# Seven products in place of eight for seven of eight k-tile pairs of up, with up and down woven job by job

## The chip, the cores and the metric

One core of one Trainium2 chip. Times are microseconds on the device from the start to the end of one execution. The kernel's matrix work is on TensorE; VectorE and ScalarE prepare its operands and take its results out of PSUM; SyncE's queue issues the loads of the weights. In rows of the profile TensorE is PE (its weight loads PEld), VectorE DVE, ScalarE ACT, SyncE SP.

## The reference

One layer over 256 tokens of width 2048, in float32: a joint projection feeds differential attention and RWKV-7 mixing, an output projection adds to the residual stream, and then the MLP, which alone the change touches:

```python
h2 = rms_norm(x, norm_mlp[l])
u = jnp.square(jax.nn.relu(jnp.einsum('btd,df->btf', h2, mlp_up[l])))
x = x + jnp.einsum('btf,fd->btd', u, mlp_down[l])
```

`mlp_up` is 2048 x 8192, `mlp_down` 8192 x 2048.

## The kernel before

**Jobs.** All weights go through one stream of jobs. A job is 256 rows of a weight matrix by 512 columns (512 KB): `load` (line 502) takes it into one of four tiles `raw`, `split` (line 517) makes two float32r tiles of it, `hi` (a cast on ScalarE) and `lo = raw - hi` (VectorE), three buffers each. A matrix product in full precision is then three float32r products: hi by hi, hi by lo, lo by hi. Two of these operands are of the activations, which are split in the same way (`hN`, `u`). The list `jobs` (lines 481 to 499) is the order in which jobs are loaded, split and used.

**A group** (`gemm`, line 571) makes 512 columns of the result for all 256 tokens. A group of up has eight jobs, a group of down four. A plain, slow job takes, for each of two k-tiles and two token tiles, three products of 512 columns: twelve.

**Fast jobs.** In groups 3 to 15 of up (`QUICK = 3`) the pairs of k-tiles in `FAST` take the 2 x 2 block form with seven products in place of eight (`seven`, line 545): the weights of a pair are four blocks of 256 columns, VectorE makes four sums and differences of them in the tile `T` (lines 533 to 535: one instruction of 512 elements, two of 256), ScalarE casts them to `Th`, VectorE makes `Tl = T - Th` of 1024, and of `lo` only 256 and 512 elements are needed. The sums of the activations, `S`, are made once, in `normal_h` (line 1449). A fast job is seven times three products of 256 columns, 21. Its partial sums lie in four banks of PSUM (b0 to b3, 512 columns each) instead of two, and `join` (line 1483) puts them together on VectorE, by way of the SBUF tiles `q` and `C`, when the group is over.

**After a group.** For up, ScalarE and VectorE apply the relu while moving 32 x 32 blocks into `z` (line 1500); `fin`, in the next group, transposes, squares and splits it into `u`. For down, VectorE adds the two banks into the residual tile `x2` (line 1393).

**Order.** Before, up and down alternate by groups: one group of up (eight jobs), two of down (four each), and so on (lines 1545 to 1549); each group takes its banks alternately from the tags `acc` and `side` (line 574), four banks each. The program is recorded, and `plan` (line 195) sets a fixed order of each engine's instructions by a list schedule: what can start first goes first, then what has the lowest rank. The rank is the place in the recording, less `SPL = 120` for `split`.

Of the kernel before, what the change touches and what calls it, by code (L numbers as in the profile page):

```python
# [21 lines left out]
P = 128  # L22
# [10 lines left out]
NRAW = 4  # L33
LOOK = 2
EV = 13
FAST = (1, 2, 4, 5, 7)
QUICK = 3

SPL = 120
# [297 lines left out]
def record(ctx, tc, A, nc):  # L337
# [37 lines left out]
    def bank(tag):  # L375
        return ps.tile([P, 512], F32, tag=tag if tag == "acc" else "side", bufs=4, name=nm(tag))
# [99 lines left out]
                advance(t)  # L476

    w_in, w_out, w_up, w_dn = A["w_in"], A["w_out"], A["up"], A["down"]
    turn = [0]

    jobs = []
    cols = [(c + 512 * h, 512) for h in range(2) for c in (4096, 3072, 5120)] + [(c + 512 * h, 512) for h in range(2) for c in (0, 1024, 2048)]
# [5 lines left out]
    def up_jobs(i):  # L488
        return [(w_up, 256 * k, 512 * i, 512) for k in range(8)]
# [1 line left out]
    def fast(job):  # L491
        return job[0] is w_up and job[2] >= 512 * QUICK and job[1] // 256 in FAST

    jobs += up_jobs(0) + up_jobs(1)
    for e in range(8):
        for j in range(4):
            if e < 7 and not j % 2:
                jobs += up_jobs(2 * e + 2 + j // 2)
            jobs += [(w_dn, e * 1024 + 256 * k, 512 * j, 512) for k in range(4)]
    raws, parts = deque(), deque()  # L500

    def load(between=None):
# [42 lines left out]
    def seven(acc, u, k, S, B, first, last):  # L545


        hi, lo, Th, Tl = B
        lt, rt = slice(0, 256), slice(256, 512)

        def a(t, kk):
            return [u[:, i, k + kk, t * P:(t + 1) * P] for i in range(2)]

        def s(i):
            return [S[:, j, i] for j in range(2)]

        def b(kk, n):
            return [x[:, kk, n * 256:n * 256 + 256] for x in (hi, lo)]

        def t(i):  # L560
            return [x[:, i] for x in (Th, Tl)]
        for n, half, x, y in ((2, lt, a(0, 0), b(0, 0)), (0, lt, a(0, 1), b(1, 0)), (0, rt, s(3), b(1, 1)), (3, lt, s(0), t(0)),
                              (3, rt, s(2), t(1)), (2, rt, s(1), t(2)), (1, lt, a(1, 1), t(3))):
            o = acc[n][:, half]
            begin = first and n > 1 and half == lt
            end = last and (n == 1 or half == rt)
            nc.tensor.matmul(o, x[0], y[0], start=begin, stop=False, skip_group_check=True)
            nc.tensor.matmul(o, x[0], y[1], start=False, stop=False, skip_group_check=True)
            nc.tensor.matmul(o, x[1], y[0], start=False, stop=end, skip_group_check=True)

    def gemm(units, w, c0, ncols, evac, side=False, hooks={}, off=0):
        turn[0] += w is w_up or w is w_dn
        quick = [j for j in range(8) if fast((w, 256 * j, c0))]
        acc = [bank("side" if turn[0] % 2 else "acc") for _ in range(4 if quick else 2)]
        nu = 4 if w is not w_out and w is not w_dn else 2
        nh = 2 * nu
        for j in range(nh):
            assert jobs[pos[2]][0] is w and jobs[pos[2]][2:] == (c0, ncols)
            pos[2] += 1
            hi, lo, *T_ = parts.popleft()  # L580
            split()
            if j in hooks:
                hooks[j]()
            if side:
                pump(BD * ncols / 512, BA * ncols / 512)
            if j in quick:
                seven(acc, units[j // 2], 2 * j % 4, sums_[FAST.index(j)], (hi, lo, *T_), j == quick[0], j == quick[-1])
                done(2)
                continue
            for kk in range(2):  # L590
                k = 2 * j + kk
                u = units[off + j // 2]
                for t in range(2):
                    xh = u[:, 0, k % 4, t * P:(t + 1) * P]
                    xl = u[:, 1, k % 4, t * P:(t + 1) * P]
                    o = acc[t][:, :ncols]
                    more = dict(skip_group_check=True) if quick else {}
                    nc.tensor.matmul(o, xh, hi[:, kk, :ncols], start=(k == 0), stop=False, **more)
                    nc.tensor.matmul(o, xh, lo[:, kk, :ncols], start=False, stop=False, **more)
                    nc.tensor.matmul(o, xl, hi[:, kk, :ncols], start=False, stop=(k == 2 * nh - 1), **more)  # L600
        evac(acc)

    def rsqrt_small(out, ss, scale, bias):

# [827 lines left out]
        squares(x2[j], parts2, j)  # L1432

    rows2 = []

    def rstd_rows():

# [11 lines left out]
    def normal_h(j):  # L1449

        u, a = unit("hN"), hA[j]
        hN.append(u)
        for kk in range(4):
            nc.vector.scalar_tensor_tensor(a[:, kk], a[:, kk], pc("g_mlp", 4 * j + kk), rows2[0], op0=ALU.mult, op1=ALU.mult)
        nc.scalar.copy(u[:, 0], a)
        nc.vector.tensor_sub(u[:, 1], a, u[:, 0])
        for p in range(2):
            if 2 * j + p in FAST:

                S, sr = ftile([P, 2, 4, P], "S", F32R), ftile([P, 4, P], "sr")  # L1460
                a1, a2 = a[:, 2 * p], a[:, 2 * p + 1]
                nc.vector.tensor_add(sr[:, 0], a1[:, P:], a2[:, P:])
                nc.vector.tensor_sub(sr[:, 1], sr[:, 0], a1[:, :P])
                nc.vector.tensor_sub(sr[:, 2], a1[:, :P], a1[:, P:])
                nc.vector.tensor_sub(sr[:, 3], a2[:, :P], sr[:, 1])
                nc.scalar.copy(S[:, 0], sr)
                nc.vector.tensor_sub(S[:, 1], sr, S[:, 0])
                sums_.append(S)
                done()
        done()  # L1470
# [6 lines left out]
    us = []  # L1477
    pend = []

    def up_group(i, hooks):  # L1480


        def join(acc):

            C, q = ftile([P, 2, 512], "C"), ftile([P, 3, 256], "q")
            lt, rt = slice(0, 256), slice(256, 512)
            b0, b1, b2, b3 = acc
            nc.scalar.copy(q[:, 0], b2[:, lt])
            nc.vector.tensor_add(q[:, 2], q[:, 0], b2[:, rt])
            nc.vector.tensor_add(q[:, 1], q[:, 2], b3[:, lt])  # L1490
            qf = q.rearrange("p a c -> p (a c)")
            nc.vector.tensor_add(C[:, 0], qf[:, :512], b0)
            nc.vector.tensor_add(C[:, 1, lt], q[:, 2], b1[:, lt])
            nc.vector.tensor_add(C[:, 1, rt], q[:, 1], b1[:, rt])
            nc.vector.tensor_add(C[:, 1, lt], C[:, 1, lt], b3[:, rt])
            nc.vector.tensor_add(C[:, 1, rt], C[:, 1, rt], b3[:, rt])
            done()
            return C

        def f(acc):  # L1500
            z = ftile([P, 4, 2, 4, 32], "z")
            C = join(acc) if i >= QUICK else None
            for t in range(2):
                for tb in range(4):
                    rows = slice(32 * tb, 32 * tb + 32)
                    src = (C[:, t] if C is not None else acc[t]).rearrange("p (f c i) -> p f c i", c=4, i=32)
                    for cb in range(4):
                        o, s = z[32 * cb:32 * cb + 32, :, t, tb, :], src[rows, :, cb, :]
                        r = rstd2[rows, t:t + 1]
                        if 4 * tb + cb < EV:  # L1510
                            nc.scalar.activation(o, s, AF.Relu, **({} if i > 1 else dict(scale=r)))
                        elif i > 1:
                            nc.vector.tensor_scalar(o, s, 0.0, None, op0=ALU.max)
                        else:
                            nc.vector.tensor_scalar(o, s, r, 0.0, op0=ALU.mult, op1=ALU.max)
            if C is not None:
                done()

            def fin():
                u = unit("u")  # L1520
                us.append(u)
                uf = ftile([P, 4, T], "uf")
                nc.vector.transpose(uf.rearrange("p f t -> p (f t)"), z.rearrange("p f t b i -> p (f t b i)"))
                nc.scalar.activation(uf, uf, AF.Square)
                nc.scalar.copy(u[:, 0], uf)
                nc.vector.tensor_sub(u[:, 1], uf, u[:, 0])
                done(2)
            pend.append(fin)
        gemm(hN if i > 1 else hT, w_up, 512 * i, 512, f, hooks=hooks)

    def store_evac(j):
        def f(acc):
# [6 lines left out]
        while pend:  # L1539
            pend.pop(0)()  # L1540

    up_group(0, {2: lambda: make_h(3), 4: rstd_rows})
    up_group(1, {2 * j: lambda j=j: normal_h(j) for j in range(4)})
    done()
    for e in range(8):
        for j in range(4):
            if e < 7 and not j % 2:
                up_group(2 * e + 2 + j // 2, {1: fin_hook})
            gemm(us, w_dn, 512 * j, 512, store_evac(j) if e == 7 else add_evac(x2[j]), hooks={1: fin_hook}, off=2 * e)


def _constants(par):
# [87 lines left out]
```

## Time and profile before

| | us |
|---|---|
| median of 3 runs | 1191.91 (1191.9 to 1193.7) |
| the profiled execution | 1192.01 |
| its span in the trace | 1190.2 |
| TensorE busy | 1179.4 (99%) |
| VectorE busy | 974.1 (82%) |
| ScalarE busy | 844.8 (71%) |

The span is from the first to the last instruction of the program; the execution's time has 1.8 us more around it. Busy time is the union of an engine's records. Records of TensorE and VectorE overlap their successors, so the price of an instruction in a dense run is the distance from its start to the next one's. The weight stream begins with the projections; group 0 of up follows at about 490 us, and from there to the end the MLP runs. All instructions have the line of the helper that emits them (L334), so they are told apart by the tiles they write and read.

### The profile page before, as it was taken

How to read it: one execution, taken by the hardware profiler on the slowest of the kernel's cores; microseconds unless marked ns; L12 is line 12 of the kernel's file. 1: busy time of each engine (PE TensorE's matmuls, PEld its weight loads, DVE VectorE, ACT ScalarE, POOL GpSimd, SP SyncE). 2: the span in 40 equal slices, each digit the busy share in tenths (PEclk: the TensorE clock that was granted, in tenths of full speed). 3: DMA queues.
4: the chain of work that ended last, by engine and by line, in shares of the span. 5: the costliest groups of instructions: out<-in, count | busy, mean ns of one | idle time of the engine just before them, and what ended most of it. 6: DMA issues, size and time to landing. Idle time of an engine off the chain costs nothing.

```text
span 1190.2 us, 18141 instructions
## 1 busy us (share of the span) xinstructions
PE 1179.4 (99%) x6649; PEld 979.9 (82%) x6649; DVE 974.1 (82%) x1579; ACT 844.8 (71%) x1421; POOL 7.3 (1%) x31
## 2 busy tenths in 40 slices
PE   9999999999999999999999999999999999999998
PEld 6887887888778778788888888888888888888886
DVE  7789594896975976798988988988988998898864
ACT  7784566855687768999686777687677677677652
POOL 2000000000000000000000000000000000000000
PEclk9999999999999999999999999999999999999999
DMA  8655656256455445656666666666666666666663
GB/s 279 205 159 164 172 162 184 85 165 175 128 169 172 141 142 184 180 169 194 188 198 199 184 203 198 194 190 197 212 176 196 198 192 182 208 180 197 207 205 132
DMA packets 126297, 216.20 MB, mean 182 GB/s; under 512 B 21824, under 2 KB 24384, under 8 KB 126208
## 3 DMA queue, kind: packets, MB, share of 16 engines
q1 hardware_dynamic: 126208, 215.05, 60.0%
q8 instruction: 52, 0.85, 0.3%
q14 instruction: 37, 0.30, 0.1%
HBM read 211.09 MB, written 3.93 MB: 181 GB/s over the span
## 4 chain that ended last, share of the span: by engine, by line
PE 77%; DVE 10%; ACT 7%; DMA 3%; issue 3%; SPq 0%; DVEq 0%; ACTq 0%
PE acc L334 47%; PE side L334 23%; DVE lo L334 4%; PE sm L334 3%; PE tr L334 3%; ACT z L334 2%; ACT hi L334 2%; DVE Tl L334 2%; DVE T L334 2%; PE sm L179 2%; DMA raw<-up 1%; DMA raw<-w_in 1%; DVE x L334 1%; DVE uf L334 0%; DVE u L334 0%
## 5 line engine op out<-in xcount | busy, mean ns | idle before, releaser
L334 DVE TENSOR_TENSOR lo<-raw,hi 128x1024 fp32r<-128x1024 f32 (+3 forms) x460 | 462.7, 1015 | 151.3 <-ACT hi L334 148.7
L334 ACT CAST hi<-raw 128x1024 fp32r<-128x1024 f32 (+2 forms) x395 | 405.0, 1033 | 164.2 <-PE acc L334 106.8
L334 PE MATMUL acc<-hi,xT 128*128 128x512 f32 (+1 forms) x832 | 267.6, 396 | 0.6 <-ACT hi L334 0.6
L334 PEld LDWEIGHTS acc<-hi,xT 128*128 128x128 f32 x832 | 154.6, 190 | 33.8 <-ACT hi L334 1.7
L334 PE MATMUL acc<-lo,xT 128*128 128x512 f32 (+1 forms) x416 | 164.0, 394 | 0.7 <-DVE lo L334 0.6
L334 PE MATMUL acc<-hi,u 128*128 128x512 f32 x512 | 163.2, 395 | 0.0
L334 PE MATMUL side<-hi,u 128*128 128x512 f32 x512 | 163.1, 395 | 0.0
L334 ACT ACTIVATE z<-C 32x128 f32<-32x128 f32 x338 | 104.2, 308 | 39.4 <-DVE C L334 35.0
L334 ACT CAST Th<-T 128x1024 fp32r<-128x1024 f32 x65 | 68.2, 1050 | 71.0 <-DVE T L334 70.3
L334 PEld LDWEIGHTS acc<-hi,u 128*128 128x128 f32 x512 | 96.4, 188 | 22.4 <-DVE u L334 0.3
L334 PEld LDWEIGHTS side<-hi,u 128*128 128x128 f32 x512 | 96.5, 188 | 22.2
L334 PE MATMUL side<-lo,u 128*128 128x512 f32 x256 | 101.0, 395 | 0.0
L334 PE MATMUL acc<-lo,u 128*128 128x512 f32 x256 | 101.0, 394 | 0.0
L334 PEld LDWEIGHTS acc<-lo,xT 128*128 128x128 f32 x416 | 78.9, 190 | 18.2 <-DVE lo L334 2.2
L334 PE MATMUL side<-hi,hN 128*128 128x512 f32 (+1 forms) x328 | 91.7, 353 | 0.0
L334 PE MATMUL acc<-hi,hN 128*128 128x512 f32 (+1 forms) x308 | 83.4, 343 | 0.0
L334 DVE TENSOR_TENSOR Tl<-T,Th 128x1024 fp32r<-128x1024 f32 x65 | 79.1, 1216 | 0.0
L334 PEld LDWEIGHTS side<-hi,hN 128*128 128x128 f32 x328 | 59.7, 188 | 9.5
L334 PEld LDWEIGHTS acc<-hi,hN 128*128 128x128 f32 x308 | 55.5, 188 | 7.8
L334 PE MATMUL side<-lo,hN 128*128 128x512 f32 (+1 forms) x164 | 57.9, 353 | 0.0
L334 PEld LDWEIGHTS acc<-lo,u 128*128 128x128 f32 x256 | 48.2, 188 | 11.0
L334 PEld LDWEIGHTS side<-lo,u 128*128 128x128 f32 x256 | 48.2, 188 | 11.0
(310 smaller groups left out, 1874.0 us busy)
## 6 DMA issues: line engine op xcount, KB each, us to landing
raw<-up SPq DMA_DIRECT2D x128, 512.0 KB, 3.8
raw<-down SPq DMA_DIRECT2D x128, 512.0 KB, 4.4
raw<-w_in SPq DMA_DIRECT2D x93, 512.0 KB, 3.8
raw<-w_out SPq DMA_DIRECT2D x32, 512.0 KB, 3.9
raw<-w_in SPq DMA_DIRECT2D x8, 288.0 KB, 3.1
x<-x SPq DMA_DIRECT2D x4, 512.0 KB, 7.3
out<-x SPq DMA_DIRECT2D x8, 256.0 KB, 3.4
raw<-w_in SPq DMA_DIRECT2D x6, 256.0 KB, 5.8
```

Of the source, the lines that this page charges most:

```text
L179: p.fn(*p.args, **p.kw)
L334: op.fn(*op.args, **op.kw)
```

## The change

`FAST` grows from five pairs to seven (only pair 0 stays slow). `gemm` becomes a generator, `steps`, which yields after each job, so that two groups can be recorded in turns. From group 3 of up on, the eight jobs of a group of up and the eight of two groups of down follow the string `WEAVE`; down groups lag by one pair less than before, and six of them are left for the end in place of four. All groups of up but the second take their banks from `acc`, all of down from `side`. In `join` two adds of 256 become one of 512, and its instructions get the rank of `split`. `normal_h` makes seven `S`; the first two lie in small tiles that the earlier stages have done with (`HOME`).

```diff
-FAST = (1, 2, 4, 5, 7)
+FAST = (1, 2, 3, 4, 5, 6, 7)
...
-    jobs += up_jobs(0) + up_jobs(1)
-    for e in range(8):
-        for j in range(4):
-            if e < 7 and not j % 2:
-                jobs += up_jobs(2 * e + 2 + j // 2)
-            jobs += [(w_dn, e * 1024 + 256 * k, 512 * j, 512) for k in range(4)]
+    def down_jobs(d):
+        return [(w_dn, d // 4 * 1024 + 256 * k, d % 4 * 512, 512) for k in range(4)]
+
+
+    WEAVE = "ddududuududududu"
+    for i in range(3):
+        jobs += up_jobs(i)
+    for i in range(3, 16):
+        ups, downs = up_jobs(i), down_jobs(2 * i - 6) + down_jobs(2 * i - 5)
+        jobs += [(ups if c == "u" else downs).pop(0) for c in WEAVE]
+    for d in range(26, 32):
+        jobs += down_jobs(d)
...
-    def gemm(units, w, c0, ncols, evac, side=False, hooks={}, off=0):
-        turn[0] += w is w_up or w is w_dn
+    def gemm(*args, **kw):
+        for _ in steps(*args, **kw):
+            pass
+
+    def steps(units, w, c0, ncols, evac, side=False, hooks={}, off=0, tag="acc"):
         quick = [j for j in range(8) if fast((w, 256 * j, c0))]
-        acc = [bank("side" if turn[0] % 2 else "acc") for _ in range(4 if quick else 2)]
+        acc = [bank(tag) for _ in range(4 if quick else 2)]
...
+            if j < nh - 1:
+                yield
         evac(acc)
+        yield
...
+            nc.rank = -SPL
             nc.scalar.copy(q[:, 0], b2[:, lt])
...
-            nc.vector.tensor_add(C[:, 1, lt], C[:, 1, lt], b3[:, rt])
-            nc.vector.tensor_add(C[:, 1, rt], C[:, 1, rt], b3[:, rt])
+            c1 = C[:, 1].rearrange("p (n c) -> p n c", n=2)
+            nc.vector.tensor_add(c1, c1, b3[:, rt].unsqueeze(1).broadcast_to([P, 2, 256]))
+            nc.rank = 0
...
+    def down_group(d):
+        e, j = d // 4, d % 4
+        return steps(us, w_dn, 512 * j, 512, store_evac(j) if e == 7 else add_evac(x2[j]), hooks={1: fin_hook}, off=2 * e, tag="side")
...
+    for i in range(3, 16):
+        gens = {"u": up_group(i, {}), "d": run(down_group(2 * i - 6), down_group(2 * i - 5))}
+        for c in WEAVE:
+            next(gens[c])
+    for _ in run(*(down_group(d) for d in range(26, 32))):
+        pass
```

Where instructions stand now, on VectorE. First, two fast jobs in the middle of a group of up, before (each row: line, operation, tile written and tiles read, shape):

```order
L334 TENSOR_TENSOR T_1395<-raw_1370 128x512
L334 TENSOR_TENSOR Tl_1388<-T_1386,Th_1387 128x1024
L334 TENSOR_TENSOR lo_1391<-raw_1367,hi_1390 128x1024
L334 TENSOR_TENSOR T_1395<-raw_1370,T_1395 128x256
L334 TENSOR_TENSOR lo_1394<-raw_1370,hi_1393 128x256
L334 TENSOR_TENSOR T_1395<-raw_1370,T_1395 128x256
L334 TENSOR_TENSOR lo_1394<-raw_1370,hi_1393 128x512
L334 TENSOR_TENSOR T_1401<-raw_1373 128x512
L334 TENSOR_TENSOR lo_1400<-raw_1373,hi_1399 128x256
L334 TENSOR_TENSOR T_1401<-raw_1373,T_1401 128x256
L334 TENSOR_TENSOR lo_1400<-raw_1373,hi_1399 128x512
L334 TENSOR_TENSOR Tl_1397<-T_1395,Th_1396 128x1024
```

And at the like place in the change:

```order
L334 TENSOR_TENSOR T_1431<-raw_1408 128x512
L334 TENSOR_TENSOR lo_1430<-raw_1408,hi_1429 128x256
L334 TENSOR_TENSOR T_1431<-raw_1408,T_1431 128x256
L334 TENSOR_TENSOR lo_1430<-raw_1408,hi_1429 128x512
L334 TENSOR_TENSOR T_1431<-raw_1408,T_1431 128x256
L334 TENSOR_TENSOR lo_1436<-raw_1414,hi_1435 128x1024
L334 TENSOR_TENSOR T_1440<-raw_1419 128x512
L334 TENSOR_TENSOR Tl_1433<-T_1431,Th_1432 128x1024
L334 TENSOR_TENSOR T_1440<-raw_1419,T_1440 128x256 x2
L334 TENSOR_TENSOR lo_1439<-raw_1419,hi_1438 128x256
L334 TENSOR_TENSOR lo_1439<-raw_1419,hi_1438 128x512
L334 TENSOR_TENSOR lo_1445<-raw_1425,hi_1444 128x1024
```

Before, two fast jobs' T, lo and Tl follow one another; now the lo of a job of down (128x1024, `raw` and `hi` read) stands between them. Next, the end of a group of up, before:

```order
L334 TENSOR_TENSOR lo_1418<-raw_1398,hi_1417 128x1024
L334 TENSOR_TENSOR lo_1426<-raw_1404,hi_1425 128x1024
L334 TENSOR_TENSOR q_1422<-q_1422,side_1382 128x256
L334 TENSOR_TENSOR q_1422<-q_1422,side_1383 128x256
L334 TENSOR_TENSOR C_1421<-q_1422,side_1381 128x256
L334 TENSOR_TENSOR C_1421<-q_1422,side_1380 128x512
L334 TENSOR_TENSOR C_1421<-q_1422,side_1381 128x256
L334 TENSOR_TENSOR C_1421<-C_1421,side_1383 128x256 x2
L334 TENSOR_TENSOR lo_1429<-raw_1407,hi_1428 128x1024
```

And in the change:

```order
L334 TENSOR_TENSOR q_1452<-q_1452,acc_1383 128x256
L334 TENSOR_TENSOR T_1469<-raw_1443 128x512
L334 TENSOR_TENSOR q_1452<-q_1452,acc_1384 128x256
L334 TENSOR_TENSOR C_1451<-q_1452,acc_1382 128x256
L334 TENSOR_TENSOR C_1451<-q_1452,acc_1381 128x512
L334 TENSOR_TENSOR C_1451<-q_1452,acc_1382 128x256
L334 TENSOR_TENSOR T_1469<-raw_1443,T_1469 128x256
L334 TENSOR_TENSOR C_1451<-C_1451,acc_1384 128x512
```

The last adds into C are one instruction of 512, the four banks are all of `acc`, and the T of the next group's first fast job is worked in. Third, the rows that follow these in the change:

```order
L334 TENSOR_TENSOR lo_1459<-raw_1437,hi_1458 128x1024
L334 TENSOR_TENSOR T_1469<-raw_1443,T_1469 128x256
L334 TENSOR_TENSOR T_1478<-raw_1449 128x512
L334 TENSOR_TENSOR T_1478<-raw_1449,T_1478 128x256
L334 TENSOR_TENSOR lo_1468<-raw_1443,hi_1467 128x256
L334 TENSOR_TENSOR lo_1468<-raw_1443,hi_1467 128x512
L334 TENSOR_TENSOR Tl_1471<-T_1469,Th_1470 128x1024
L334 TENSOR_TENSOR T_1478<-raw_1449,T_1478 128x256
L334 TENSOR_TENSOR T_1484<-raw_1457 128x512
```

The four tiles `raw` are used in turn: raw_1457 is loaded four loads after raw_1437 (1437, 1443, 1446, 1449, 1457), into the same place, which the first row here reads last; the last row is the first to read the new one.

## Rows read from the trace of the kernel before

**Rows 1.** Page, first and second part: TensorE's busy time; granted clock by slices.

```profile
PE 1179.4 (99%) x6649; PEld 979.9 (82%) x6649; DVE 974.1 (82%) x1579; ACT 844.8 (71%) x1421; POOL 7.3 (1%) x31
...
PEclk9999999999999999999999999999999999999999
```

**Rows 2.** Stretches: us; busy PE, PEld, DVE, ACT, POOL (instructions); clock, DMA share, GB/s.

```profile
635.10:1068.40 433.30, 432.88 (x2372) 373.33 (x2370) 385.35 (x601) 314.72 (x501) 0.00 (x0) 1.00 0.64 194
...
744.20:770.00 25.80, 25.72 (x156) 22.72 (x155) 25.73 (x40) 16.94 (x19) 0.00 (x0) 1.00 0.62 181
...
770.00:787.00 17.00, 17.00 (x82) 14.12 (x81) 12.23 (x20) 13.86 (x32) 0.00 (x0) 1.00 0.68 215
...
508.00:545.00 37.00, 37.00 (x160) 29.98 (x160) 35.87 (x68) 35.06 (x67) 0.00 (x0) 1.00 0.61 180
```

**Rows 3.** TensorE's timeline: start, us, engine, line, product, shape, count.

```profile
755.87 0.28 PE L334 MATMUL acc<-hi,hN 128*128 128x256 f32 x1
...
758.37 0.39 PE L334 MATMUL acc<-hi,hN 128*128 128x512 f32 x1
...
764.68 0.28 PE L334 MATMUL acc<-Th,S 128*128 128x256 f32 x1
...
765.04 0.39 PE L334 MATMUL acc<-Tl,S 128*128 128x256 f32 x1
...
769.34 0.28 PE L334 MATMUL acc<-lo,hN 128*128 128x256 f32 x1
...
771.69 0.40 PE L334 MATMUL side<-hi,u 128*128 128x512 f32 x1
...
782.84 0.40 PE L334 MATMUL acc<-hi,u 128*128 128x512 f32 x1
```

**Rows 4.** VectorE's timeline, same columns; idle time before and its releaser.

```profile
757.68 0.42 DVE L334 TENSOR_TENSOR T<-raw,T 128x256 f32<-128x256 f32 x1
...
758.01 0.69 DVE L334 TENSOR_TENSOR lo<-raw,hi 128x512 fp32r<-128x512 f32 x1
...
758.62 0.69 DVE L334 TENSOR_TENSOR T<-raw 128x512 f32<-128x512 f32 x1
...
764.90 1.22 DVE L334 TENSOR_TENSOR lo<-raw,hi 128x1024 fp32r<-128x1024 f32 x1
...
766.03 0.42 DVE L334 TENSOR_TENSOR T<-raw,T 128x256 f32<-128x256 f32 x1
...
787.05 0.69 DVE L334 TENSOR_TENSOR T<-raw 128x512 f32<-128x512 f32 x1 [0.82 <-DMA raw<-up]
```

**Rows 5.** VectorE's groups, 635.1 to 1068.4 us: busy, mean ns, idle before.

```profile
L334 DVE TENSOR_TENSOR lo<-raw,hi 128x1024 fp32r<-128x1024 f32 x111 | 134.4, 1218 | 38.7 <-ACT hi L334 38.1
...
L334 DVE TENSOR_TENSOR T<-raw,T 128x256 f32<-128x256 f32 x100 | 41.8, 418 | 0.3
...
L334 DVE TENSOR_SCALAR z<-C 32x128 f32<-32x128 f32 x60 | 13.3, 222 | 1.3
...
L334 DVE STREAM_TRANSPOSE uf<-z 128x1024 f32<-128x1024 f32 x10 | 12.4, 1238 | 0.0
```

**Rows 6.** Waits, 635.1 to 1068.4 us: us in total, times, longest.

```profile
DVE lo L334 <- ACT hi L334: 38.1, 46, 1.8
...
ACT hi L334 <- PE side L334: 13.7, 15, 1.3
...
ACT hi L334 <- PE acc L334: 13.4, 15, 1.3
...
DVE T L334 <- DMA raw<-up: 7.2, 10, 0.9
```

**Rows 7.** ScalarE's groups, 635.1 to 1068.4 us.

```profile
L334 ACT CAST Th<-T 128x1024 fp32r<-128x1024 f32 x50 | 52.5, 1050 | 51.9 <-DVE T L334 51.3
```

**Rows 8.** Page, sixth part: transfers, KB each, median us from issue to landing.

```profile
raw<-up SPq DMA_DIRECT2D x128, 512.0 KB, 3.8
...
raw<-down SPq DMA_DIRECT2D x128, 512.0 KB, 4.4
```

More of the change, by code (lines that the diff above doesn't have):

```diff
@@ L478, in record @@
     w_in, w_out, w_up, w_dn = A["w_in"], A["w_out"], A["up"], A["down"]
-    turn = [0]
     jobs = []
@@ L554, in s @@
         def s(i):
-            return [S[:, j, i] for j in range(2)]
+            return [S[j][:, i] for j in range(2)]
         def b(kk, n):
@@ L588, in gemm @@
                 done(2)
-                continue
-            for kk in range(2):
+            for kk in range(0 if j in quick else 2):
                 k = 2 * j + kk
@@ L1434, in record @@
     rows2 = []
+    HOME = {0: ("DW", "DA"), 1: ("X", "Sp")}
     def rstd_rows():
@@ L1458, in normal_h @@
             if 2 * j + p in FAST:
-                S, sr = ftile([P, 2, 4, P], "S", F32R), ftile([P, 4, P], "sr")
+                sr = ftile([P, 4, P], "sr")
+                if len(sums_) in HOME:
+                    S = [sm.tile([P, 512], F32R, tag=g, bufs=1, name=nm("S")).rearrange("p (s t) -> p s t", s=4) for g in HOME[len(sums_)]]
+                else:
+                    S = ftile([P, 2, 4, P], "S", F32R)
+                    S = [S[:, 0], S[:, 1]]
                 a1, a2 = a[:, 2 * p], a[:, 2 * p + 1]
@@ L1465, in normal_h @@
                 nc.vector.tensor_sub(sr[:, 3], a2[:, :P], sr[:, 1])
-                nc.scalar.copy(S[:, 0], sr)
-                nc.vector.tensor_sub(S[:, 1], sr, S[:, 0])
+                nc.scalar.copy(S[0], sr)
+                nc.vector.tensor_sub(S[1], sr, S[0])
                 sums_.append(S)
@@ L1478, in record, with up_group @@
     pend = []
-    def up_group(i, hooks):
+    def up_group(i, hooks, tag="acc"):
         def join(acc):
@@ L1528, in f @@
             pend.append(fin)
-        gemm(hN if i > 1 else hT, w_up, 512 * i, 512, f, hooks=hooks)
+        return steps(hN if i > 1 else hT, w_up, 512 * i, 512, f, hooks=hooks, tag=tag)
     def store_evac(j):
@@ L1540, in fin_hook, with run @@
             pend.pop(0)()
-    up_group(0, {2: lambda: make_h(3), 4: rstd_rows})
-    up_group(1, {2 * j: lambda j=j: normal_h(j) for j in range(4)})
-    done()
[L1545 to L1549, printed above, removed]
+    def down_group(d):
+        e, j = d // 4, d % 4
+        return steps(us, w_dn, 512 * j, 512, store_evac(j) if e == 7 else add_evac(x2[j]), hooks={1: fin_hook}, off=2 * e, tag="side")
+    def run(*gens):
+        for g in gens:
+            yield from g
+    for _ in run(up_group(0, {2: lambda: make_h(3), 4: rstd_rows}),
+                 up_group(1, {2 * j: lambda j=j: normal_h(j) for j in range(4)}, "side")):
+        pass
+    done()
+    for _ in up_group(2, {1: fin_hook}):
+        pass
+    for i in range(3, 16):
[3 more added lines that the diff above has]
+    for _ in run(*(down_group(d) for d in range(26, 32))):
+        pass
 def _constants(par):
```

## The prediction

> **What bounds the kernel now.** Read the page's first part, then the table by stretches, then TensorE's and VectorE's timelines, then the waits. [...] But the next engine is not far behind: over ten whole periods of the MLP (a period is one group of up and two of down, 16 jobs) VectorE is busy 385.35 of 433.3 us, ScalarE 314.72 [rows 2]. One period takes 43.33 us, of which VectorE works 38.5. It is not even: in the stretch from 744.2 to 770.0, where the five fast jobs of a group stand together, VectorE is busy for 25.73 of 25.8 us; in the next 17 us, under the two groups of down, for 12.23 [rows 2].
>
> TensorE's price of a job is read from starts, since records overlap. A down group of 48 products of 512 columns starts at 771.69 and the next begins at 782.84 [rows 3]: 11.15 us, 0.232 a product, 2.79 a job of twelve. A fast job of 21 products of 256 runs from 755.87 to 758.37, 2.50; from the second product of another, 769.34, to the end of its group at 771.69 are 2.35 for twenty, 2.47 for 21 [rows 3]. I use 2.48, 0.118 a product. 11 slow and 5 fast jobs make 43.09 us; the period is 43.33, so about 0.24 is stall. It is seen where the fast jobs have used up VectorE's lead: the step from 764.68 to 765.04 is 0.36 instead of 0.12 [rows 3].
>
> VectorE too is read from starts: 256 elements step by 0.33, 512 by 0.61, 1024 by 1.13 [rows 4]. A fast job issues T (512), T, T (256 each), lo (256 and 512), Tl (1024): 0.61 + 3 x 0.335 + 0.61 + 1.13 = 3.35 us, against 2.48 on TensorE. A slow job has one lo, 1.13 against 2.79. So VectorE falls behind in up and recovers in down, and its idle time is there: 38.1 us in ten periods waiting for hi, while ScalarE's hi waits 27.1 us for TensorE to give back a hi buffer [rows 6]. That is an engine up to three jobs ahead, with nothing to do.
>
> **The change part by part.** (1) *Two more jobs of each of 13 groups go by seven products.* TensorE saves 2 x (2.79 - 2.48) = 0.62 us a period, 8.1 in all, on the path. The period's floor on TensorE becomes 9 x 2.79 + 7 x 2.48 = 42.47.
>
> [...] The rows show a product of 256 columns at half the price of one of 512, with no fixed part that can be seen [rows 3]. [...]
>
> (2) *VectorE pays for it.* Per converted job lo of 1024 goes and Tl of 1024 comes, so the thousands cancel; added are T and lo of 512 and three of 256: 2 x 0.61 + 3 x 0.335 = 2.22, 4.45 a period. (3) *The join's last two adds become one* of 512: 0.61 for 2 x 0.33, a gain of 0.06. VectorE's work in a period was 38.5 by busy time. By steps it is 17 of 1024 (11 lo, five Tl, one u) x 1.13 = 19.2, 15 of 512 (five T, five lo, four x, one C) x 0.61 = 9.2, 21 of 256 (ten T, five lo, two q, four C) x 0.335 = 7.0, and the transpose and six z at 1.24 + 1.33 [rows 5]: 38.0. Busy time is higher because each dense run ends in a full record. After: 17, 20 and 25 of them, 42.4 by steps, 42.9 by busy time. **VectorE then needs as much as TensorE**, 42.4 against 42.47, and what idles it is on the path.
>
> (4) *The weave.* It adds no work. It sets a lo of 1.13 beside each fast job, 4.48 us of VectorE for 5.27 of TensorE, so that the lead isn't used up in a run of fast jobs; that is what makes 42.4 us of work fit at all. With the lead even, the 0.24 of stall goes, and its place is taken by whatever makes VectorE wait. (5) *ScalarE* gains two Th of 1.05 [rows 7], 2.1 on 31.5 of 43.3: covered by the ten idle us that are left, and Th waited for VectorE 51.9 us in ten periods, so it is not what is late. (6) *The banks.* Every group of up now takes all four banks of acc, so the next group waits for the join. The two down jobs that open a period give 2 x 2.79 = 5.6 us. Between the last fast product and the last read of the first two banks stand one ScalarE copy of 256 columns, under the 1.05 of a cast of 1024 [rows 7], and by the order two q, a T and three C, 2 x 0.335 + 0.61 + 2 x 0.335 + 0.61 = 2.6: 3.6 us at most, covered by 2.0; if the join begins later than that, TensorE stands. (7) *Two more sums of h.* At most 4 x 0.335 + 0.61 = 1.95 each on VectorE, 3.9 together, before the third group of up. From 508 to 545 VectorE had 1.1 us free [rows 2]; the eight slow jobs after that leave it 8 x (2.79 - 1.13). Price 0 to 2; with thirteen free us behind it I take nothing.
>
> (8) *The transfers.* Here is the cost that the trace of before doesn't show. T reads a job's raw tile early, lo reads it last and frees it, and there are four. VectorE waits for raw once a period now, 7.2 us in ten [rows 6], 0.82 at 787.05 [rows 4], where it is idle anyway. In the new order the tightest place is the third piece of VectorE's order above: from the end of lo on the tile four loads earlier to the T that needs the new one stand three T and one lo of 256, T and lo of 512, and one Tl, 4 x 0.335 + 2 x 0.61 + 1.13 = 3.69 us, and the transfer needs 3.8 for up, 4.4 for down from issue to landing [rows 8]. So VectorE waits between 0.1 and 0.7 there; nothing if it stood elsewhere in between. I take 0.35 a period.
>
> **Sum.** VectorE 42.4 + 0.35 = 42.75 us a period against 43.33: 0.58 x 13 = 7.5 us. From the profiled execution's 1192.0 (the median of the runs shown is 0.1 below): **1184.5 us**. At best TensorE's floor holds: 0.86 x 13 = 11.2, about 1180 with rounding. With VectorE at 42.9 and 0.2 of waits it is 0.23 x 13 = 3.0 less, 1189.
>
> **Rivals.** *The raw tiles starve VectorE; slower.* With no idle time left, every late landing counts. Four T of a period have under 5 us of VectorE work to cover their transfer, by the same counting 3.7, 4.4, 4.9 and 5.0. If the landing, in a stream that now changes between two matrices, takes 5.2 us in place of 3.8 to 4.4, those four wait 1.5 + 0.8 + 0.3 + 0.2 = 2.8, less what one wait gives the next, an estimate of 2 us: 44.4 a period, 1.07 x 13 = 14 us more, 1206. It decides at 0.93 us of VectorE idle a period (43.33 - 42.4). For it: landing is already longer than the cover at one place. Against: the queue has moved 512 KB per 2.7 us all along with the DMA engines busy 64% [rows 2]. Chance 0.11.
>
> *Given back; no change.* VectorE's small waits (ScalarE's hi, Th, the join's copy) add up to 0.75 to 1.1 us a period. For it: a static order has to meet two engines at 100%. Against: the dense stretch of 25.8 us with no gap [rows 2]. 1190 to 1194; 0.2%, 2.4 us, is what a measurement of this kernel can tell from no change. Chance 0.08.
>
> *Records, not steps, are VectorE's price; slower.* If each instruction held the engine for its whole record (1.22 for 1024, where the next starts after 1.13 [rows 4]), the work would be 17 x 1.22 + 20 x 0.69 + 25 x 0.42 + 2.6 = 47.6 us a period, 4.3 x 13 = 56 us more, 1248. [...] Chance 0.01.
>
> *Small products cost more between long ones; no change.* Now products of 256 and 512 columns change over every job, not every few. At 2.79 / 21 = 0.133 a product instead of 0.118 a fast job saves nothing. Against: both runs of fast products that gave 2.50 and 2.47 end in such a change [rows 3]. [...] Chance 0.01.
>
> That the change doesn't do what it says is excluded: the order shows the lo of down jobs between the T of up jobs.
>
> **How the numbers follow.** Forecast 0.79, all of it faster by over 0.2%, 1180 to 1189; no change 0.09; slower 0.12. Leaving out the slower cases and a little below the floor: 1179 to 1192.
>
> **What would show it.** Right: periods of 42.5 to 43.0 us, VectorE busy 98% or more in them, few waits of lo for hi, and T waiting for raw as VectorE's main wait. TensorE's steps should be 0.232 and 0.118 as before, with stalls of a few tenths before Tl and lo. Wrong: VectorE idle by over 0.9 us a period, TensorE waiting before the first product of a group of up (the join), or ScalarE's hi late with its buffers free.

## The result, and the profile after

The changed kernel takes **1198.95 us** (median of 6 runs, 1198.2 to 1201.9) against 1191.97 for the kernel before on the same chip: a ratio of 1.0061, 95% interval 1.0047 to 1.0075. It is slower by 7 us, where 7.5 us less was forecast. One of the six executions of the kernel before took 3705.71 us; the ratio goes by the others. The profiled execution's span is 1196.8 us, before 1190.2.

The page's first part of the change, busy times:

```profile
PE 1172.5 (98%) x6883; PEld 983.1 (82%) x6883; DVE 1034.6 (86%) x1706; ACT 875.2 (73%) x1449; POOL 7.3 (1%) x31
```

The table by stretches over ten whole periods of the change, columns as in [rows 2]:

```profile
666.30:1103.80 437.50, 428.16 (x2552) 377.32 (x2550) 429.78 (x691) 336.33 (x521) 0.00 (x0) 1.00 0.62 193
```

A period takes 43.75 us, before 43.33 [rows 2]. VectorE works 42.98 of them, 98.2%, before 38.5; TensorE's clock is whole throughout (1.00). So VectorE is as full as forecast, but TensorE's periods did not get shorter. TensorE's timeline at one place of each period:

```profile
709.35 0.28 PE L334 MATMUL acc<-Tl,hN 128*128 128x256 f32 x1
709.47 0.28 PE L334 MATMUL acc<-Th,hN 128*128 128x256 f32 x1
709.58 0.63 PE L334 MATMUL side<-hi,u 128*128 128x512 f32 x2
711.13 0.50 PE L334 MATMUL side<-lo,u 128*128 128x512 f32 x1 [0.91 <-DVE lo L334]
711.46 0.39 PE L334 MATMUL side<-hi,u 128*128 128x512 f32 x1
711.70 0.39 PE L334 MATMUL side<-lo,u 128*128 128x512 f32 x1
```

Products of 256 columns step by 0.12 and of 512 by 0.23, as in [rows 3]; from 709.58 two products should last 0.46 us, and the third starts after 1.55. It waits for the `lo` of the down job that follows the two neighbouring fast jobs of `WEAVE` ("uu"). The same stall stands in every one of these periods, 1.0 to 1.4 us with the step after it. What VectorE does before it, from its timeline:

```profile
699.54 1.22 DVE L334 TENSOR_TENSOR Tl<-T,Th 128x1024 fp32r<-128x1024 f32 x1
700.77 0.22 DVE L334 TENSOR_SCALAR z<-C 32x128 f32<-32x128 f32 x1
701.02 0.43 DVE L334 TENSOR_TENSOR T<-raw,T 128x256 f32<-128x256 f32 x1
...
704.79 1.22 DVE L334 TENSOR_TENSOR Tl<-T,Th 128x1024 fp32r<-128x1024 f32 x1
705.92 0.42 DVE L334 TENSOR_TENSOR T<-raw,T 128x256 f32<-128x256 f32 x1
706.26 0.68 DVE L334 TENSOR_TENSOR x<-x,side 128x512 f32<-128x512 f32 x1
706.96 0.22 DVE L334 TENSOR_SCALAR z<-C 32x128 f32<-32x128 f32 x1
707.19 0.43 DVE L334 TENSOR_TENSOR T<-raw,T 128x256 f32<-128x256 f32 x1
707.63 0.46 DVE L334 TENSOR_SCALAR z<-C 32x128 f32<-32x128 f32 x2
708.12 0.69 DVE L334 TENSOR_TENSOR x<-x,side 128x512 f32<-128x512 f32 x1
708.73 1.24 DVE L334 STREAM_TRANSPOSE uf<-z 128x1024 f32<-128x1024 f32 x1
709.89 1.19 DVE L334 TENSOR_TENSOR lo<-raw,hi 128x1024 fp32r<-128x1024 f32 x1
```

And ScalarE's timeline there:

```profile
704.50 3.19 ACT L334 ACTIVATE z<-C 32x128 f32<-32x128 f32 x10
707.71 2.00 ACT L334 CAST hi<-raw 128x1024 fp32r<-128x1024 f32 x2
```

VectorE has no gap here; the `lo` at 709.89 comes after six `z` and the transpose. One `z` steps by 0.23 to 0.25, and an instruction ahead of a run of `z` steps 0.1 longer: `Tl` to `z` is 1.23 where `Tl` to `T` is 1.13, `x` to `z` 0.70 where `x` to `uf` is 0.61. Six `z` in four runs cost 0.25 + 0.49 + 0.23 + 0.49 + 4 x 0.1 = 1.86 us (the second run stands at 702.42, not shown). The planner (`plan`, which fixes the order) has a table of costs that gives a `z` 0.068 + 128 x 0.00052 = 0.135, 0.81 for six. VectorE's steps here are not in proportion to the elements: four steps of 256 elements would be 4 x 0.335 = 1.34 us, where one of 1024 is 1.13, and a `z` of 128 takes 0.235.

The change's waits from 650 to 1070 us (in total, times, longest):

```profile
ACT hi L334 <- PE side L334: 56.3, 33, 2.8
...
PEld side L334 <- DVE lo L334: 13.7, 10, 1.6
PE side L334 <- DVE lo L334: 9.3, 10, 1.1
...
DVE lo L334 <- ACT hi L334: 3.9, 9, 0.4
...
DVE T L334 <- DMA raw<-up: 0.2, 1, 0.2
```

And the page's sixth part, median us from issue to landing last:

```profile
raw<-up SPq DMA_DIRECT2D x128, 512.0 KB, 4.5
raw<-down SPq DMA_DIRECT2D x128, 512.0 KB, 4.0
```

`T` waiting for raw, forecast as VectorE's main wait, is all but gone, though tiles of up land later than in [rows 8]. VectorE's own idle time, 0.77 us a period, is for more than half a wait of `lo` for `hi` (4.4 of 7.7 us in the ten periods). That `hi` had waited for TensorE to give back one of three buffers, as VectorE's timeline and then ScalarE's show at one place:

```profile
730.75 2.36 DVE L334 TENSOR_TENSOR lo<-raw,hi 128x1024 fp32r<-128x1024 f32 x2 [0.44 <-ACT hi L334]
```

```profile
729.67 2.12 ACT L334 CAST hi<-raw 128x1024 fp32r<-128x1024 f32 x2 [2.21 <-PE side L334]
```

So the engines wait for each other by turns: TensorE is late, `hi` and `lo` are then late, and what VectorE has lost there it lacks at the next "uu".

Summed over all of TensorE's starts from 440 us on (each distance beyond 0.118 or 0.232, if by more than 0.03), the stalls are 21.0 us, before 6.3: 7.3 against 3.0 up to 650, and 13.6 against 3.3 from there. The products save 8.1. 14.7 - 8.1 = 6.6 us, the difference of the two spans. Of the 4.3 more up to 650, 2.2 stand between 550 and 560, where the first down group waits for `u` (TensorE's timeline below), 1.3 at 570, where a fast job waits, and 2.0 at 621, the same `lo` after "uu" in the second woven period; some 1.2 of stalls that the kernel before had between 575 and 600 are gone:

```profile
553.61 0.40 PE L334 MATMUL acc<-hi,hN 128*128 128x512 f32 x1
555.02 0.50 PE L334 MATMUL side<-hi,u 128*128 128x512 f32 x1 [1.02 <-ACT u L334]
...
556.52 0.73 PE L334 MATMUL side<-hi,u 128*128 128x512 f32 x2 [0.76 <-DVE u L334]
```

### The profile page after: what moved, and what is told of

Same layout as the page of the kernel before. It is cut to its first block, busy times and chain, and to the rows that moved or that the text cites. A ratio compares the mean times of both kernels' runs of the same rounds, so it can differ in the third digit from the quotient of the medians.

```text
span 1196.8 us, 18805 instructions
## 1 busy us (share of the span) xinstructions
PE 1172.5 (98%) x6883; PEld 983.1 (82%) x6883; DVE 1034.6 (86%) x1706; ACT 875.2 (73%) x1449; POOL 7.3 (1%) x31
## 4 chain that ended last, share of the span: by engine, by line
PE 65%; DVE 21%; ACT 7%; issue 5%; DMA 3%; SPq 0%; DVEq 0%; ACTq 0%
PE acc L334 37%; PE side L334 21%; DVE lo L334 8%; DVE T L334 3%; ACT hi L334 3%; PE tr L334 2%; DVE Tl L334 2%; PE sm L334 2%; DMA raw<-up 2%; PE sm L179 2%; DVE C L334 1%; ACT z L334 1%; DVE z L334 1%; DVE uf L334 1%; DVE x L334 1%
## 5 line engine op out<-in xcount | busy, mean ns | idle before, releaser
L334 PE MATMUL side<-hi,u 128*128 128x512 f32 x1024 | 336.5, 395 | 1.8 <-ACT u L334 1.0
L334 PEld LDWEIGHTS side<-hi,u 128*128 128x128 f32 x1024 | 191.9, 188 | 42.6 <-ACT u L334 1.5
L334 PE MATMUL side<-lo,u 128*128 128x512 f32 x512 | 203.3, 397 | 11.8 <-DVE lo L334 11.8
L334 PE MATMUL acc<-hi,hN 128*128 128x256 f32 (+1 forms) x532 | 134.8, 317 | 0.8 <-DVE z L334 0.8
L334 ACT CAST Th<-T 128x1024 fp32r<-128x1024 f32 x91 | 95.2, 1047 | 25.0 <-DVE T L334 24.5
L334 PE MATMUL acc<-Th,S 128*128 128x256 f32 x546 | 112.3, 281 | 0.0
L334 PEld LDWEIGHTS acc<-Th,S 128*128 128x128 f32 x546 | 90.2, 188 | 0.0
L334 PE MATMUL acc<-lo,hN 128*128 128x256 f32 (+1 forms) x266 | 84.3, 317 | 0.0
L334 DVE TENSOR_TENSOR T<-raw,T 128x256 f32<-128x256 f32 x182 | 76.7, 422 | 1.7
L334 PE MATMUL acc<-Tl,S 128*128 128x256 f32 x273 | 77.2, 283 | 0.0
L334 DVE TENSOR_TENSOR T<-raw 128x512 f32<-128x512 f32 x91 | 62.5, 687 | 1.6 <-DMA raw<-up 1.3
```

The lines of the kernel that those rows point to most:

```text
L334: op.fn(*op.args, **op.kw)
```

## The experiments

Stalls below are such sums over TensorE's starts, up to 650 us / from there. In kernels with added lines the helper stands at L338.

| kernel | us | ratio to before, 95% | stalls |
|---|---|---|---|
| change | 1198.95 | 1.0061 (1.0047 to 1.0075) | 7.3 / 13.6 |
| weave5 | 1200.88 | 1.0072 (1.0057 to 1.0087) | 4.5 / 9.5 |
| weave6 | 1213.64 | 1.0182 (1.0167 to 1.0197) | 6.7 / 24.5 |
| plain7 | 1236.63 | 1.0374 (1.0357 to 1.0391) | 12.9 / 45.0 |
| finlate | 1209.87 | 1.0146 (1.0120 to 1.0171) | 8.0 / 20.3 |
| rank_hi | 1197.12 | 1.0038 (1.0024 to 1.0053) | 5.6 / 13.4 |
| uuend | 1199.62 | 1.0060 (1.0045 to 1.0075) | 8.4 / 14.5 |
| uuend_rank | 1200.80 | 1.0066 (1.0049 to 1.0083) | 7.2 / 16.6 |
| weave5_rank | 1200.49 | 1.0069 (1.0045 to 1.0093) | 4.2 / 10.6 |
| meas_z | 1198.97 | 1.0063 (1.0050 to 1.0075) | 5.6 / 15.5 |
| meas_l | 1202.62 | 1.0089 (1.0075 to 1.0103) | 6.6 / 17.8 |
| meas_zl | 1190.97 | 0.9995 (0.9986 to 1.0004) | 7.6 / 5.7 |
| meas_z2l | 1188.70 | 0.9975 (0.9964 to 0.9985) | 5.7 / 4.6 |
| head_s | **1187.60** | 0.9965 (0.9953 to 0.9978) | 4.8 / 5.5 |
| weave5_zl | 1193.47 | 1.0018 (1.0009 to 1.0026) | 3.4 / 3.8 |
| weave6_zl | 1194.87 | 1.0029 (1.0018 to 1.0041) | 4.7 / 7.9 |
| before_zl | 1194.89 | 1.0029 (1.0018 to 1.0040) | 3.0 / 6.0 |
| end_13 | 1188.58 | 0.9973 (0.9963 to 0.9983) | 4.8 / 5.7 |
| end_15 | 1196.39 | 1.0036 (1.0024 to 1.0049) | 4.9 / 12.5 |

**Is VectorE's load the cause?** Three kernels set the number of fast pairs and the order apart: the weave with five pairs and with six, and (plain7) the kernel before with seven pairs and seven `S`, in its order of whole groups.

```diff
-    FAST = (1, 2, 3, 4, 5, 6, 7)
+    FAST = (1, 2, 4, 5, 7)            # weave5
+    FAST = (1, 2, 3, 4, 5, 7)         # weave6
```

> The weave alone: the changed kernel with the five fast pairs of before (1, 2, 4, 5, 7). Theory A, VectorE is full (its 43.0 us of work and 0.75 of idle make the period of 43.75): with 2 x 2.2 us less on VectorE TensorE bounds, 11 x 2.79 + 5 x 2.48 = 43.1 a period, stalls below 0.3, so as before (43.33) or 2 to 3 us better, plus what the start of the weave costs (about 3 us): 1190 to 1194. Theory B, one lo comes late because blocks of z on ScalarE and the transposition uf on VectorE stand ahead of it: the place stays, with a stall near 1.25 a period: 44.3 a period, about 1207.

> One fast pair less than the change, pair 6, whose job lies behind the place of the stall in the period. Theory A (VectorE full): VectorE needs 40.8 us, TensorE 10 x 2.79 + 6 x 2.48 = 42.8, so TensorE bounds: a period of 42.8 to 43.0, stall under 0.3, about 1186 to 1190. Theory B (the late lo alone): VectorE's work ahead of the place is unchanged, the stall of 1.25 stays, period 44.0, about 1202.

> Seven fast pairs in before's order of whole groups (the two more sums of h where the change puts them, before's join). Theory A: VectorE's work is the same 42.5 to 43 us a period, but seven fast jobs in a row need 23.5 us of it for 17.4 of TensorE, and three jobs of lead don't cover 6.1 us: 45 to 47 us a period, 1213 to 1240. If the total alone counted, as in the change: about 1199.

weave5 gives VectorE back the work of two pairs and is no faster than the change; its time lies between what the two theories gave. Its stall stands at the same `lo`, 0.3 to 1.2 us a period. What is new is a wait of `T` for raw at the head of the period, ahead of the rest of the join. SyncE's timeline shows the issue, VectorE's the wait, and the waits from 650 to 1070 us the sum:

```profile
860.88 0.37 SPq L334 DMA_DIRECT2D raw<-up  x1
```

```profile
865.79 0.69 DVE L334 TENSOR_TENSOR T<-raw 128x512 f32<-128x512 f32 x1 [1.14 <-DMA raw<-up]
866.40 0.41 DVE L334 TENSOR_TENSOR q<-q,acc 128x256 f32<-128x256 f32 x1
```

```profile
DVE T L334 <- DMA raw<-up: 29.3, 18, 2.9
```

The tile came 4.9 us after its issue; the planner counts 1.1 + 524288 / 360000 + 0.9 = 3.5. Whatever stands behind that `T` in VectorE's fixed order, the join and by it all `z`, is then 1.1 us late. So a lighter VectorE alone does not help: theory A falls as the sole cause, and the weave costs some 8 us even with five pairs. weave6 is slower by 12 us than either theory allowed; its stall too stands mostly at that `lo`, 1.1 to 1.8 us a period. plain7, as theory A expected, shows what seven pairs cost without the weave, 45 us.

**Is it the work ahead of that one `lo`?** finlate holds the transpose and what follows it for the second down group; rank_hi lets the `split` of woven jobs go before other work; uuend moves the two neighbouring fast jobs to the period's end; uuend_rank has both of the last two edits, weave5_rank has rank_hi's with five pairs.

```diff
+    def held_fin():
+        nc.hold = True
+        fin_hook()
+        nc.hold = False
...
-            nc.rank = -SPL
+            nc.rank = -(SPL if pos[1] <= 160 else 1000)
...
-    WEAVE = "ddududuududududu"
+    WEAVE = "ddududududududuu"
```

> The change with uf, its square and the split into u held back to the second group of down in a period, so that they no longer stand ahead of the lo that TensorE waits for; the work is the same. Theory A: VectorE stays full, a period of 43.0 at best, no more than 0.75 a period better: 1189 to 1198. Theory B: the stall goes, period 42.5 to 42.8, 1183 to 1187.

> The change with the rank of split lowered from -120 to -1000 from the first woven job on, so that whenever a hi, lo, T, Th or Tl can start it goes ahead of z, x, uf and u; the work is the same. Theory C (the first half of a period is overfull: join, z, x, uf and u stand ahead of the parts of the next jobs on ScalarE and VectorE, and a lead of at most three jobs doesn't carry TensorE over it): the order gets better, the stall of 1.25 a period falls to 0.5 or less, 1186 to 1191. Theory D (the fixed order meets the chip's times badly wherever VectorE and ScalarE are near full, whatever goes first): as the change or worse, 1197 to 1212.

> The change with the two neighbouring jobs of up moved from the middle of WEAVE to its end (dd ud ud ud ud ud ud uu). Theory C: the overfull first half loses one fast job's 3.35 us of VectorE in exchange for a lo of 1.13, so the stall there goes; at the end VectorE has no join to do: stall under 0.5 a period, 1186 to 1191. Theory D: the stall comes back at another place, 1197 to 1212.

> Both of the two edits before. Theory C: at or near TensorE's floor where VectorE's 43.0 us allow it, 43.0 a period, 1186 to 1190. Theory D: 1197 to 1212.

> The weave with five fast pairs and the lower rank. VectorE has 4.8 us of slack a period here. Theory C: stall under 0.2, 43.2 a period, 1190 to 1193 with about 2.5 us lost at the start of the weave. Theory D: as the weave with five, 1199 to 1202.

All five stay at 1197 us or above. finlate is slower than either of its theories had it; at 752 us twelve `z` on ScalarE still stand ahead of the `hi` there. rank_hi and uuend move the stall elsewhere, to `Tl` of fast jobs, and its sum stays at 13 to 14.5 us; the waits from 650 to 1070 us of rank_hi:

```profile
PEld acc L334 <- DVE Tl L334: 7.6, 9, 0.9
```

So it is not one unlucky place, and theory D is right for the four kernels that it was set against.

**Do the planner's prices cause it?** The order is fixed before the run by durations in the planner's table. meas_z raises the price of `z` to 0.285, near the rows above, and that of the transpose from 1.13 to 1.24, the length of its record, though it steps by 1.16 there (708.73 to 709.89). meas_l raises the landing of a tile from 3.5 to 4.5, meas_zl does all of it; "both prices" below are VectorE's and the landing. The instructions stay the same; only their order moves.

```diff
+            if fname == "tensor_scalar" and aps[0].shape[0] == 32:
+                self.cost += 0.15
+            if fname == "transpose":
+                self.cost += 0.11
...
-            done = dma + 0.9
+            done = dma + (1.9 if op.ins[0].tensor.name in ("up", "down") else 0.9)
```

> Same work as the change; only two prices by which the kernel's planner lays the fixed order are set to what the trace of the change shows: a z block on VectorE (32x128) 0.28 us in place of 0.135 (it steps by 0.235, and each run of them delays its neighbours by about 0.1), the transpose 1.24 in place of 1.13. Theory E: six z in a period cost VectorE some 1.1 us more than the order allows, all of it ahead of the one lo that has no slack in that order (the down job after the two neighbouring fast jobs), and TensorE's stall of 1.25 us a period is that. An order that knows the price puts other work there: stall below 0.5 a period, period 42.8 to 43.2, total 1187 to 1193. Rival A' (VectorE is simply full: 43.0 us of busy time in a period, whatever the order): stall moves but stays, 43.5 to 43.8, total 1196 to 1200.

> The change with one price of the planner corrected, that of the landing (1.0 us later for tiles of up and down); the z keep their price. Theory L (the order counts on raw tiles that come about 1 us too early; VectorE and ScalarE stand in front of them with other work behind): 1189 to 1193, as meas_zl. Theory ZL (both prices are needed, since VectorE is at 98% and each of the two uses up the slack that the other leaves): 1194 to 1198.

> As meas_z, and the planner also counts the landing of a raw tile 1.0 us later (traces: 4.0 to 4.9 us from issue to landing; the planner counts about 3.5). Theory E: in the change T waited for raw for only 0.2 us in ten periods, so the landing is no cause there: within 2 us of meas_z. If landing matters once the z are priced right, meas_zl is faster than meas_z by 2 us or more.

One price alone gives nothing, or less than nothing; both together give 8 us. The waits from 650 to 1070 us show where the stall went. With `z` alone corrected (meas_z, first rows), VectorE waits for raw, which it did not in the change, where it came late anyway, and TensorE's stall goes over in the main to `hi` and `Th` of fast jobs; with the landing alone (meas_l, second rows), `lo` is as late as before:

```profile
DVE T L338 <- DMA raw<-up: 8.3, 9, 1.4
PEld acc L338 <- ACT hi L338: 5.5, 10, 0.7
...
PEld acc L338 <- ACT Th L338: 3.9, 6, 0.7
...
PEld side L338 <- DVE lo L338: 2.4, 4, 0.7
```

```profile
PEld side L334 <- DVE lo L334: 14.2, 10, 1.4
PE side L334 <- DVE lo L334: 12.1, 10, 1.2
...
DVE T L334 <- DMA raw<-up: 0.8, 2, 0.5
```

Theory E, which held `z` to be enough in the change, falls. Rival A' (VectorE is full whatever the order) has the time of meas_z, but falls with meas_zl, which has the same work. Theory ZL, that both are needed, stands, though meas_l lies 4.6 us above its range. The same two prices on the weave with fewer pairs:

> The weave with five fast pairs, order laid with both corrected prices. Five pairs leave VectorE over 4 us a period, and yet TensorE stalled 0.9 a period: at the head of each period a T stands first on VectorE and waits 1.2 us for raw, and all behind it, the join and the z too, comes 1.2 us late at the one lo without slack. Theory E: with the landing priced right the stall goes: period 43.1 to 43.4, total 1192 to 1195. Rival W (the weave itself costs, by banks, join or rhythm, whatever the order's prices): 1199 or more, as weave5.

> Six fast pairs (without pair 6) in the weave, order laid with both corrected prices. It was 1213.6 with the planner's own prices. Theory E: VectorE needs 40.8 of some 42.8 us, so there is slack: 1187 to 1193. Rival W: 1199 or more.

They gain 7.4 and 18.8 us, and in weave5_zl no wait of `T` for raw is left among the waits from 650 to 1070 us. weave5_zl lies where it was expected, weave6_zl 2 us above. The weave with five or six pairs stays 2 to 3.5 us slower than the kernel before. The control:

> The kernel before with the same two prices corrected, as a control. If the corrected order helps whatever the kernel, this gains too: 1186 to 1190. Theory L says that the order before, where VectorE waits for raw only under down with slack behind it and TensorE stalled 0.24 us a period, has little to win: 1190.5 to 1192.5.

The order before loses 3 us by the corrected prices (for `z` those of meas_z2l, below), more than either expectation had. They are no general cure: the new order brought 2.7 us more of stalls, of TensorE for `Tl`. That it had nothing to win because slack stood behind the waits for raw [rows 4, 6] is likely, but not shown.

**The head.** meas_zl still waits 2.4 us for `u` at 553; there `z` reads PSUM and was priced right before (its steps in meas_zl are 0.32 to 0.39, as at 566.97 and 547.55; the price was 0.36). meas_z2l raises the price for SBUF sources only; head_s lets the sums `S` go later besides.

```diff
-            if fname == "tensor_scalar" and aps[0].shape[0] == 32:
+            if single and aps[0].shape[0] == 32:
...
+                nc.rank = 100
                 sr = ftile([P, 4, P], "sr")
```

> As meas_zl, but the price of z is raised only for blocks read from SBUF; those of the first three groups of up, read from PSUM, step by 0.30 to 0.39 and were right before. In meas_zl TensorE waited 2.6 us at 553 and 1.3 at 577 for u and z of the first groups. Expected: the periods as in meas_zl (42.9 to 43.0), the head 0 to 2 us better, 1188 to 1191.

> As meas_z2l, and the sums S of the activations get a rank 100 places later, so that the split, z and u of the first groups go before them on VectorE. Theory H: the change costs about 4 us at its head (from the first job of group 1 of up to the third woven period), because seven S in place of five are made where VectorE is full; later S let the first down groups have their u in time: 1185 to 1189. Rival: the S are then late for the first fast jobs and the stall only moves: 1189 to 1192.

Both beat the kernel before, by 3 and 4 us. In meas_z2l, ten periods in the table by stretches, and its waits from 650 to 1070 us:

```profile
665.00:1094.60 429.60, 428.43 (x2552) 376.42 (x2550) 425.01 (x690) 333.57 (x521) 0.00 (x0) 1.00 0.62 196
```

```profile
PEld side L338 <- DVE lo L338: 4.0, 10, 0.5
...
DVE T L338 <- DMA raw<-up: 0.6, 2, 0.4
```

The period is 42.96 us and VectorE works 42.50 of it, 0.5 less than in the change with the same instructions: its load too depends on the order. Its `z` stand in three runs a period, in the change in four, which by the rows above is 0.1 of the 0.5; the rest is not explained.

The two intervals overlap, so that the later `S` help is not shown; the stalls up to 650 fell from 5.7 to 4.8, and 3.0 would be as before. But they moved: between 550 and 560, where the first down group waits for `u`, they fell from 2.1 to 0.1 us, and between 560 and 575 they rose from 0.8 to 2.2. The rival to theory H is right for the most part.

**What keeps the last 0.5 us a period?** end_13 is head_s with the neighbouring fast jobs at the end; end_15 differs from it only in four of six `z` that ScalarE takes over.

```diff
-                        if 4 * tb + cb < EV:
+                        if 4 * tb + cb < (EV if i < 3 else 15):
```

> As head_s, with the two neighbouring fast jobs at the end of the period. VectorE has the same work. With both prices right the place of the pair should not matter, since VectorE is the bound: within 2 us of head_s, 1186 to 1190. As uuend against the change (1199.6 and 1198.95).

> As end_13, with four of the six z blocks on VectorE in each period moved to ScalarE from group 3 of up on: VectorE loses 4 x 0.235 and the 0.1 beside each run of them, about 1.1 us a period, ScalarE gains 1.3 on 32.7. If VectorE's load is what keeps the period at 42.96 above TensorE's 42.47 once the order is right, the period falls to 42.5 to 42.7 and the total to 3 to 6 us under end_13. If the rest of the stall is lateness of single transfers or of ScalarE, it stays within 1 us of end_13 or gets worse.

end_13 came as expected: with both prices right the place of the pair doesn't matter, as it did not in uuend. end_15 is slower by 8 us though VectorE has 11 us more of idle time from 650 to 1070 us (busy for 404.29, in end_13 for 415.73). Its stretch and its waits:

```profile
650.00:1070.00 420.00, 414.52 (x2455) 362.86 (x2454) 404.29 (x628) 338.88 (x549) 0.00 (x0) 1.00 0.62 193
```

```profile
PEld acc L338 <- DVE Tl L338: 9.0, 20, 1.2
...
DVE T L338 <- DMA raw<-up: 5.5, 8, 1.3
```

So that VectorE's load is what holds the period at 42.96 is not shown; a lighter VectorE under another order waits again for raw, and TensorE for `Tl`. Every change of a price or of the work lays a new order, and the luck of each order is worth some us. What speaks against luck in the prices is that each of the four woven kernels that was laid both ways gains: 8.0 us (change to meas_zl), 7.4 and 18.8 (five and six pairs), and 11.0 (uuend to end_13, which has the later `S` too); and that all four kernels with seven pairs and both prices and six `z` on VectorE (meas_zl, meas_z2l, head_s, end_13) lie at 1187.6 to 1191.0, and the five that have seven pairs in a weave without both (change, rank_hi, uuend, uuend_rank, finlate) at 1197.1 to 1209.9, as do meas_z and meas_l. No kernel was laid with prices put off the other way, which would tell what a new order alone is worth.

## Why the prediction was wrong, point by point

**(1) held.** Products of 256 columns stepped by 0.118 among products of 512 as well; 8.1 us are saved. The rival of dearer small products is out.

**(2) held in the higher of its two numbers.** VectorE's busy time is 42.98 us a period; by busy time 42.9 was forecast, by steps 42.4. The steps left out that an instruction ahead of a run of `z` takes 0.1 longer: six `z` cost 1.86 in place of 1.33. The sum took the lower number, 0.5 us a period too little for this order. The rival that whole records are VectorE's price, 47.6, is out.

**(3), (5) and (6) held.** No stall of TensorE stands at the first product of a group of up. ScalarE works 33.6 us a period, the 31.5 + 2.1 of the forecast.

**(4) is the step that failed**: "With the lead even, the 0.24 of stall goes, and its place is taken by whatever makes VectorE wait." The lead is not even. In the order as laid, one `lo` a period comes behind all the `z`, the transpose and two of the residual's adds, and TensorE stalls there by 1.0 to 1.4 us a period, where 0.24 stood before. The prediction counted work against time over the whole period and took for granted that a fixed order meets it. That order was laid with a `z` at 0.135 and a landing at 3.5 us; the trace of the change has 0.31 with the neighbours' share, and medians of 4.0 (down) and 4.5 (up). Before, 38.5 of 43.33 us of VectorE's work left room for such errors; at 42.98 of 43.75 there is little left, and what comes late at TensorE comes back by the three buffers of `hi` as idle time of VectorE. With both prices corrected and the same instructions the period is 42.96 (meas_z2l), 0.2 above the forecast 42.75. Of its signs of being wrong, an idle VectorE (0.77 us a period, not over 0.9) and a wait at the first product of a group of up did not appear; what failed to come was its sign of being right, stalls of "a few tenths before Tl and lo". The rival *Given back* ("a static order has to meet two engines at 100%") is nearest to what happened; it stopped at 1194.

**(7) failed by its size.** "I take nothing" for two more `S`. At the first down group, TensorE stalls for `u` by 2.2 us more than before; weave5, with five `S`, has none of it, nor has head_s, where the `S` come later. The other 2.1 of the 4.3 up to 650 us are not theirs: 2.0 is the `lo` of (4) at 621. The free time that was meant to cover the sums lies in part behind the first down job, at 555, which needs `u` before. (Down groups lag by one pair more than before, not less, as "The change" has it: six in place of four are left for the end. The first of them still follows group 2 of up directly.)

**(8) named the wrong wait.** `T` waited 0.2 us for raw in 420 us, not 0.35 a period. The late transfers act through the order: weave5 and meas_z show the wait where VectorE is early enough to meet it. The rival that raw starves VectorE has the right transfer, but its landing of 5.2 us did not come (median 4.5), nor its wait, nor its 1206.

By terms, from 1192.0: products -8.1, more stalls up to 650 us +4.3 (about half of it of (7)), from there +10.4 (of (4)), which is 1198.6 against 1198.95 measured (1198.8 in the profiled execution).

## What to carry to other kernels

Where an order is fixed ahead by a table of durations, compare the table with the trace before loading an engine to 98%: errors that did little with slack can become stalls, and they can hide one another: here, correcting either alone gained nothing. Bring work and time together not per period only, but at the place where the consumer needs each operand. And a lighter engine in a new order is not a clean test of its load: the order has changed too. Where a forecast takes extra work as covered, look at what stands right behind it: there the sums of (7) held up `u`.

## What the runs showed that was not expected

A wait of TensorE was followed by more than its own cost. In meas_zl, after 8 us of dense work at full clock, TensorE waited 2.4 us for `u`; then seven products of 512 columns stepped by 0.43 in place of 0.23, at a granted clock of 0.50. TensorE's timeline, and the stretches before and after:

```profile
553.21 0.40 PE L338 MATMUL acc<-hi,hN 128*128 128x512 f32 x1
556.00 0.50 PE L338 MATMUL side<-hi,u 128*128 128x512 f32 x1 [2.39 <-ACT u L338]
...
557.29 1.05 PE L338 MATMUL acc<-hi,hN 128*128 128x512 f32 x2
558.14 1.48 PE L338 MATMUL side<-hi,u 128*128 128x512 f32 x3
```

```profile
545.00:553.00 8.00, 8.00 (x37) 6.46 (x36) 7.81 (x14) 6.76 (x14) 0.00 (x0) 1.00 0.65 195
...
556.80:559.90 3.10, 3.10 (x9) 2.32 (x8) 2.88 (x4) 3.00 (x7) 0.00 (x0) 0.50 0.40 104
```

Seven steps of 0.43 cost 7 x 0.2 = 1.4 us more. But the wait alone does not decide it. meas_z has one as long at the same place (2.45 us idle up to 556.1) and kept the whole clock behind it (first row below). uuend_rank has the two shorter waits that the change has there, 0.99 and 0.76 us, and fell (second row), where the change kept a clock of 1.00. The stalls of 1.0 to 1.4 us in the change's periods were not followed by it either. What does decide is open.

```profile
556.10:559.90 3.80, 3.80 (x16) 3.03 (x17) 3.57 (x5) 3.71 (x6) 0.00 (x0) 1.00 0.45 136
```

```profile
556.80:559.90 3.10, 3.10 (x10) 2.38 (x9) 3.08 (x5) 2.88 (x6) 0.00 (x0) 0.53 0.40 116
```

Such stretches are in weave6 (2.5 us of its 24.5), finlate (two, 2.8 of its 20.3) and plain7 too, so that a part of their stalls is the clock's.

The landing of a tile of up went from 3.8 us [rows 8] to 4.5 with the same bytes and a DMA share of 0.62 in place of 0.64, and back to 4.0 to 4.2 in meas_zl and meas_z2l and 3.8 in meas_z, at shares of 0.60 to 0.62. No run here shows what moves it.
